# Constant matmuls ahead of the first projection, another order of the first loads, and the norm of x inside a later tile

## The chip, the cores and the metric

The kernel runs on one core of one Trainium2 chip. The metric is the device time of one execution in microseconds (us); several executions are timed, and one more is taken with the hardware profiler. The engines are TensorE (PE, with its weight loads as PEld), VectorE (DVE), ScalarE (ACT), GpSimd (POOL), and SyncE (SP), which issues most transfers.

## The reference, cut to what matters

One encoder block over 512 tokens of 1024 channels. What the change touches is the normalisation of x and the projections that follow it:

```python
def rms_norm(x, g):
    y = xf * lax.rsqrt(jnp.mean(xf * xf, axis=-1, keepdims=True) + EPS)
    return y * g
...
h = rms_norm(x, mix_norm_g[l])
proj = h @ w_in[l]      # mLSTM q, k, v, o, gates | NA q, k, v | memory q | merge gates
...
qk = silu(dwconv3(concat([q_pre, k_pre]), w_conv, b_conv))   # mLSTM branch
```

The rest of the block (mLSTM, neighbourhood attention, attention into 256 memory tokens, gated merge, output projection, a convolutional feed-forward and a last norm) is computed by both kernels alike. All inputs and outputs are float32.

## The kernel before

x is kept transposed: eight k tiles of 128 channels by 512 tokens. Each float32 matmul is made of three in a rounded format (`mm3`, lines 181 to 184): an operand is split into a high part (a rounded copy) and a low part (the difference), and high*high, high*low and low*high are summed in PSUM. `split_act` (186) makes the parts of an activation: the high part on ACT (188), the low part on DVE (189). `emit_split` (153) does so for a block of weights: ACT at 164, DVE at 165. A weight block is up to 1088 columns; `emit_raw` (135) loads it into one of three buffers by SP, and `weights` (170) loads three blocks ahead and splits one ahead. The high and low halves have four buffers each.

The norm is not applied to x before the projection. Only the gain is (`vcol("mix_g", k)`, from the tile `vec`, in which all small vectors stand side by side in 180 columns); the factor per token, 1/rms, is applied to the projection's result. It is formed in two steps. `rstd_cols` (244) reduces the accumulated squares `acc` over partitions by matmuls with a column of ones (249), and takes the power -1/2 on POOL (253); the result is a column `rc`, token by partition. `rstd_row` (256) spreads it over all partitions: eight scalings of the identity on DVE (266), two matmuls (267), and a copy by ACT (269), the tile `rb`.

The start of the program, in source order: SP loads x tile 0, `vec`, block 0 in three pieces (columns 0 to 127, to 511, to 1023; line 142), x tiles 1 to 3, block 1 whole (144); POOL loads `gb`, a small bias; POOL makes constants, and DVE two halved vectors from late columns of `vec` (`mgbh` 239, `ngh` 241). Then comes the loop over the eight k tiles of the first projection, "mlq" (292 to 305): per k tile the twelve matmuls of four feature tiles, each with a PSUM bank of the pool `mm` (`ps_q`). `x_part(k)` (280) splits x tile k, squares it on ACT (283, 286), adds the square to `acc` on POOL (287), and loads x tile k+4. At k = 6 `rstd_cols` is placed ahead of the matmuls, at k = 7 `rstd_row` behind the first feature tile's.

Then four rounds of `conv` (311) and `silu2` (322) treat the four q tiles: DVE multiplies by `rb` (315), ACT and DVE apply the three taps (317 to 319), ACT a tanh (324), DVE 325, and a split. The four feature tiles of k ("mlk") follow, each a `proj` (328) of 24 matmuls into a bank of `mm`, with the same treatment. Next are the token-major blocks ("tm", 369 to 391), whose first and third rounds use the four banks of the second PSUM pool, `at`. The scratch tiles `scr`, seven buffers, hold x tiles, squares and intermediate results.

The source order is not the order on an engine. A scheduler at build time places each instruction on its engine's queue; each queue then runs in order, and each instruction waits for its own inputs.

Of the kernel before, what the change touches and what calls it, by code (L numbers as in the profile page):

```python
# [11 lines left out]
F32 = mybir.dt.float32  # L12
F32R = mybir.dt.float32r
AF = mybir.ActivationFunctionType
# [3 lines left out]
P = 128  # L18
S = 512
D = 1024  # L20
KT = D // P
# [3 lines left out]
FT = DFF // P  # L25
HF = FT // 2
NU = 15
RM, RB = 0.75, 1.4
RATE = (0.85, 1.6, 0)
EPS = 1e-6  # L30
# [65 lines left out]
def hybrid_block(ctx, tc, xT, memT, wflat, vecs, gbias, nabias, outa, outb):  # L96
    nc = tc.nc
    V, A, G, PE, SY = nc.vector, nc.scalar, nc.gpsimd, nc.tensor, nc.sync

    cp = ctx.enter_context(tc.tile_pool(name="cp", bufs=1))  # L100
    wp = ctx.enter_context(tc.tile_pool(name="wp", bufs=3))
    up = ctx.enter_context(tc.tile_pool(name="up", bufs=NU))
    sp = ctx.enter_context(tc.tile_pool(name="sp", bufs=7))
# [7 lines left out]
    def nm(s):  # L111
        uid[0] += 1
        return f"{s}_{uid[0]}"
# [4 lines left out]
    def scr(n=512):  # L118
        return sp.tile([P, 516], F32, tag="scr", name=nm("s"))[:, :n]

    def tiny(n):
        return tp.tile([P, 32], F32, tag="tiny", name=nm("y"), bufs=12)[:, :n]

    def mmps():
        return mmp.tile([P, 512], F32, tag="mm", name=nm("mm"))

    def atps():
        return atp.tile([P, 512], F32, tag="at", name=nm("at"))
# [4 lines left out]
    st = {"raw": 0, "split": 0}  # L133

    def emit_raw(i):
        key, n = BLOCKS[i]
        _, off, _ = BINDEX[key]
        r = wp.tile([P, BW], F32, tag="raw", name=nm("wr"), bufs=3)
        src = wflat[off:off + P * n].rearrange("(p n) -> p n", p=P)
        if i == 0:  # L140
            for a, b in ((0, P), (P, n // 2), (n // 2, n)):
                SY.dma_start(r[:, a:b], src[:, a:b])
        else:
            SY.dma_start(r[:, :n], src)
        raws[i] = r

    def halves(i):
        n, c = BLOCKS[i][1], BCOLS[BLOCKS[i][0][0]](BLOCKS[i][0])
        k = n // c
        k0 = k if n <= HWD else (k + 1) // 2  # L150
        return c, [(0, k0)] + ([(k0, k)] if k0 < k else [])

    def emit_split(i):
        key, n = BLOCKS[i]
        r = raws.pop(i)
        c, hs = halves(i)
        split[i] = []
        for a, b in hs:
            h = wp.tile([P, HWD], F32R, tag="hi", name=nm("wh"), bufs=4)
            l = wp.tile([P, HWD], F32R, tag="lo", name=nm("wl"), bufs=4)  # L160
            m = (b - a) * c
            for u, v in ((0, P), (P, m)) if i == 0 and a == 0 else ((0, m),):
                src = r[:, a * c + u:a * c + v]
                A.activation(h[:, u:v], src, AF.Copy)  # L164
                V.tensor_tensor(l[:, u:v], src, h[:, u:v].bitcast(F32), op=ALU.subtract)  # L165
            for k in range(a, b):
                q = slice((k - a) * c, (k - a + 1) * c)
                split[i].append((h[:, q], l[:, q]))

    def weights(key):  # L170

        i, _, n = BINDEX[key]
        while st["raw"] <= min(i + RAW_AHEAD, len(BLOCKS) - 1):
            emit_raw(st["raw"])
            st["raw"] += 1
        while st["split"] <= min(i + SPLIT_AHEAD, len(BLOCKS) - 1):
            emit_split(st["split"])
            st["split"] += 1
        return split.pop(i)

    def mm3(ps, lh, ll, rh, rl, start, stop):
        PE.matmul(ps, lh, rh, start=start, stop=False)  # L182
        PE.matmul(ps, lh, rl, start=False, stop=False)  # L183
        PE.matmul(ps, ll, rh, start=False, stop=stop)  # L184

    def split_act(h, l, src, scale=1.0):

        A.activation(h, src, AF.Copy, scale=scale)  # L188
        V.scalar_tensor_tensor(l, src, scale, h.bitcast(F32), op0=ALU.mult, op1=ALU.subtract)  # L189


    vec = cp.tile([P, NVEC], F32, name="vec")
    gb = cp.tile([P, 16], F32, name="gb")

    def vcol(name, i):
        o = VEC[name] + i
        return vec[:, o:o + 1]
# [3 lines left out]
    def load_x(k):  # L201
        if k < KT:
            t = scr()
            SY.dma_start(t, xT[:, k, :])
            xk.append(t)

    load_x(0)
    SY.dma_start(vec, vecs)
    emit_raw(0)
    for k in range(1, 4):  # L210
        load_x(k)
    emit_raw(1)
    st["raw"] = 2
    G.dma_start(gb, gbias.partition_broadcast(P))

    ident = cp.tile([P, P], F32, name="ident")
    make_identity(nc, ident)
# [26 lines left out]
    def rstd_cols(acc, ntok, tag, n=D):  # L244

        nt = ntok // P
        ps = atps()
        for t in range(nt):
            PE.matmul(ps[:, t:t + 1], acc[:, t * P:(t + 1) * P], ones[:, 0:1], start=True, stop=True)
        v = tiny(nt)  # L250
        V.tensor_scalar(v, ps[:, :nt], 1.0 / n, EPS, op0=ALU.mult, op1=ALU.add)
        col = cp.tile([P, nt], F32, name=f"rc_{tag}")
        G.tensor_tensor(col, v, nhalf[:, :nt], op=ALU.pow)
        return col

    def rstd_row(col, ntok, tag):

        nt = ntok // P
        ch, cl = tp.tile([P, 32], F32R, tag="tiny", name=nm("y"), bufs=12)[:, :nt], tiny(nt)
        A.activation(ch, col, AF.Copy)  # L260
        V.tensor_tensor(cl, col, ch.bitcast(F32), op=ALU.subtract)
        pb = atps()
        for n, c in enumerate((ch.bitcast(F32), cl)):
            dg = sp.tile([P, 516], F32R, tag="scr", name=nm("s"))[:, :ntok]
            for t in range(nt):
                V.tensor_scalar(dg[:, t * P:(t + 1) * P], ident, c[:, t:t + 1], None, op0=ALU.mult)
            PE.matmul(pb[:, :ntok], onesr, dg, start=n == 0, stop=n == 1)
        rb = cp.tile([P, ntok], F32, name=f"rb_{tag}", tag=f"rb{ntok}", bufs=2 if ntok == S else 1)
        A.activation(rb, pb[:, :ntok], AF.Copy)
        return rb  # L270
# [3 lines left out]
    XH = [hx[k // 4][:, (k % 4) * S:(k % 4 + 1) * S] for k in range(KT)]  # L274
    XL = [hx[2 + k // 4][:, (k % 4) * S:(k % 4 + 1) * S] for k in range(KT)]
    acc = cp.tile([P, S], F32, name="acc_x", tag="acc", bufs=1)
# [2 lines left out]

    def x_part(k):  # L280
        split_act(XH[k], XL[k], xk[k], vcol("mix_g", k))
        if k == 0:
            A.activation(acc, xk[k], AF.Square)
        else:
            sq = scr()
            A.activation(sq, xk[k], AF.Square)
            G.tensor_tensor(acc, acc, sq, op=ALU.add)
        load_x(k + 4)

    x_part(0)  # L290
    done = 1
    for k in range(KT):
        if k % 2 == 0:
            ws = weights(("mlq", k // 2))
        while done < min(KT, k + 1 + (k > 2)):
            x_part(done)
            done += 1
        if k == KT - 2:
            rc = rstd_cols(acc, S, "x")
        wh, wl = ws[k % 2]  # L300
        for f in range(4):
            fs = slice(f * P, (f + 1) * P)
            mm3(ps_q[f], wh[:, fs], wl[:, fs], XH[k], XL[k], k == 0, k == KT - 1)
            if k == KT - 1 and f == 0:
                rb = rstd_row(rc, S, "x")
    rcc = cp.tile([P, NT], F32, name="rcc")
    V.tensor_scalar(rcc, rc, C_ML, None, op0=ALU.mult)

# [16 lines left out]
        V.scalar_tensor_tensor(c, th, 1.0, c, op0=ALU.add, op1=ALU.mult)  # L325
        split_act(dst[0][:, sl], dst[1][:, sl], c)

    def proj(key, XHs, XLs, n=S):
        ws = weights(key)
        ps = mmps()  # L330
        for k in range(KT):
            mm3(ps[:, :n], ws[k][0], ws[k][1], XHs[k], XLs[k], k == 0, k == KT - 1)
        return ps

    qT = [unit(F32R), unit(F32R)]
    kT = [unit(F32R), unit(F32R)]
    for f in range(4):
        silu2(qT, slice(f * S, (f + 1) * S), conv(ps_q[f], rb, "mlw", "mlb", f, 8))
    for f in range(4):
        ps = proj(("mlk", f), XH, XL)  # L340
        silu2(kT, slice(f * S, (f + 1) * S), conv(ps, rb, "mlw", "mlb", 4 + f, 8))

    mh_u, ml_u = unit(F32R), unit(F32R)
# [25 lines left out]
    for c in range(4):  # L369
        if c == 3:  # L370
            mem_part()
        n = 272 if c == 0 else 256
        pss = [(mmps if c % 2 else atps)() for _ in range(NT)]
        for h in range(2):
            ws = weights(("tm", c, h))
            for t in range(NT):
                tsl = slice(t * P, (t + 1) * P)
                for k in range(4):
                    kk = 4 * h + k
                    ps = pss[t][:, :n]  # L380
                    mm3(ps, XH[kk][:, tsl], XL[kk][:, tsl], ws[k][0], ws[k][1], kk == 0, kk == KT - 1)
        for t in range(NT):
            ps = pss[t]
# [418 lines left out]
    for f in range(4):  # L802
        ps = proj(("xaq", f), XH, XL)
# [6 lines left out]
    for f in range(4):  # L810
        ps = proj(("o", f), XH, XL)
# [9 lines left out]
    for f in range(4):  # L821
        ps = proj(("memk", f), MH, ML, M)
# [3 lines left out]
    for i in range(4):  # L826
        ws = weights(("memv", i))
# [10 lines left out]
    for f in range(4):  # L838
        ps = proj(("naq", f), XH, XL)
# [3 lines left out]
    for f in range(4):  # L843
        ps = proj(("nak", f), XH, XL)
# [12 lines left out]
    for br in range(3):  # L857
# [8 lines left out]
        for fp in range(4):  # L866
            tg = []
            for i in range(2):
                f = 2 * fp + i
                ps = proj(("g", br, f), XH, XL)  # L870
# [9 lines left out]
            ws = weights(("br", br, fp))  # L880
            for i in range(2):
                f = 2 * fp + i
                ps = mmps()
# [22 lines left out]
    for f in range(KT):  # L906
        xr = scr()
        SY.dma_start(xr, xT[:, f, :])
        ps = proj(("out", f), GH, GL)
# [73 lines left out]
    for hh in range(2):  # L983
# [3 lines left out]
        for j in range(HF):  # L987
            f = HF * hh + j
            if f == 0:
# [7 lines left out]
                k = KT - 1  # L997
# [19 lines left out]
        for f in range(KT):  # L1017
            ws = weights(("dn", hh, f, 0)) + weights(("dn", hh, f, 1))
            last = hh == 1 and f == KT - 1
            for a, b in ((0, 256), (256, 512)) if last else ((0, 512),):  # L1020
                ps = mmps()[:, :b - a]
# [120 lines left out]
```

## Time and profile before

| | us |
|---|---|
| three timed executions | 917.39, 918.46, 918.47 (median 918.46) |
| the profiled execution | 917.16 |
| its span, first to last instruction | 915.4 |
| DVE, ACT, POOL busy in it | 577.7, 437.7, 135.0 |
| 0 to 10 us: PE busy | 4.55 |
| 10 to 880 us: PE busy | 867.2 |
| 880 to 915.4 us: PE busy | 28.0 |

A timeline row has the start, the duration (of the group, where it says x2 or more, from the first start to the last end), the engine, the line of the kernel, the operation, what it writes and reads with shapes, and, in brackets, how long the engine was idle before it and what ended that. In the rows of groups the busy time and the mean of one instruction stand before the second bar, the idle time of the engine just before them behind it. Matmul durations overlap, so the distance between two starts tells the rate. "fp32r" is the rounded format. `wr` is a raw weight block, `wh` and `wl` its parts, `s` a scratch tile, `u` a large unit tile.

### The profile page before, as it was taken

What the parts mean: (1) busy time and instruction counts of PE and PEld (TensorE: products, weight loads), DVE (VectorE), ACT (ScalarE), POOL (GpSimd) and SP (SyncE); (2) the same over time, 40 slices, a digit from 0 to 9 for tenths busy, and PEclk for the clock granted to TensorE, in tenths of its full rate; (3) what the DMA queues carried; (4) which work ended last, traced back from release to release, by engine and by line L of the source; (5) the groups of instructions that cost most, each with busy time, mean ns of one, the idle gap of its engine ahead of it and who ended that gap; (6) DMA issues with size and microseconds to landing.
All of it is one profiled execution on the core that took longest, in us unless ns stands there. A gap on an engine that the chain in (4) does not pass through costs nothing.

```text
span 915.4 us, 12086 instructions
## 1 busy us (share of the span) xinstructions
PE 899.7 (98%) x4431; PEld 750.8 (82%) x4431; DVE 577.7 (63%) x993; ACT 437.7 (48%) x879; POOL 135.0 (15%) x158
## 2 busy tenths in 40 slices
PE   7999999999999999999999999999999999999996
PEld 5899878888888888788888888888888888888886
DVE  7893665746566668895454548777733477777333
ACT  7464546655545557563334435444422344444442
POOL 6000321102040300111111221111100011111112
PEclk9999999999999999999999999999999999999999
DMA  7223522422231423232223332222222322222322
GB/s 256 96 93 106 189 98 101 155 92 90 81 127 73 134 81 125 83 127 70 93 92 116 137 116 92 92 93 93 85 95 95 115 93 92 93 93 86 95 72 92
DMA packets 32939, 96.39 MB, mean 105 GB/s; under 512 B 4056, under 2 KB 7528, under 8 KB 32880
## 3 DMA queue, kind: packets, MB, share of 16 engines
q1 hardware_dynamic: 31440, 92.45, 29.2%
q0 software_dynamic: 1440, 3.17, 1.2%
q8 instruction: 35, 0.57, 0.3%
q14 instruction: 24, 0.20, 0.1%
HBM read 92.44 MB, written 3.16 MB: 104 GB/s over the span
## 4 chain that ended last, share of the span: by engine, by line
PE 95%; DVE 2%; issue 1%; DMA 0%; ACT 0%; POOL 0%; SPq 0%; POOLq 0%; DVEq 0%; ACTq 0%
PE mm L182 28%; PE mm L183 28%; PE mm L184 28%; PE at L535 2%; PE at L182 2%; PE at L183 2%; PE at L184 2%; PE at L671 1%; PE at L658 1%; DMA wr<-wflat 0%; POOL u L979 0%; PE at L748 0%; PE at L642 0%; PE at L643 0%; DVE s L890 0%
## 5 line engine op out<-in xcount | busy, mean ns | idle before, releaser
L182 PE MATMUL mm<-u,wh 128*128 128x512 f32 (+1 forms) x1115 | 435.8, 391 | 5.4 <-ACT wh L164 5.3
L184 PE MATMUL mm<-u,wl 128*128 128x512 f32 (+1 forms) x1115 | 433.2, 389 | 0.0
L183 PE MATMUL mm<-u,wh 128*128 128x512 f32 (+1 forms) x1115 | 433.0, 388 | 0.0
L164 ACT ACTIVATE wh<-wr 128x512 fp32r<-128x512 f32 (+3 forms) x305 | 189.5, 623 | 298.4 <-PE mm L183 262.6
L165 DVE TENSOR_TENSOR wl<-wr,wh 128x512 fp32r<-128x512 f32 (+3 forms) x305 | 234.4, 770 | 145.2 <-ACT wh L164 141.0
L182 PEld LDWEIGHTS mm<-u,wh 128*128 128x128 f32 x1115 | 209.9, 188 | 50.8 <-ACT wh L164 6.2
L184 PEld LDWEIGHTS mm<-u,wl 128*128 128x128 f32 x1115 | 209.8, 188 | 45.9
L183 PEld LDWEIGHTS mm<-u,wh 128*128 128x128 f32 x1115 | 209.9, 188 | 44.8 <-DVE u L189 0.5
L1012 POOL TENSOR_TENSOR s<-s,rb 128x512 f32<-128x512 f32 x22 | 29.1, 1324 | 266.4 <-DVE s L1011 258.3
L891 POOL TENSOR_TENSOR u<-u,s 128x512 f32<-128x512 f32 x16 | 22.4, 1399 | 166.1 <-DVE s L890 108.9
L188 ACT ACTIVATE u<-s 128x512 fp32r<-128x512 f32 x34 | 21.4, 629 | 52.3 <-DVE s L1015 50.6
L872 DVE TENSOR_TENSOR s<-mm,rb_x 128x512 f32<-128x512 f32 x24 | 16.6, 692 | 28.8 <-PE mm L184 28.8
L189 DVE SCALAR_TENSOR_TENSOR u<-s,u 128x512 fp32r<-128x512 f32 x34 | 23.5, 692 | 14.7 <-ACT u L188 14.4
L523 ACT ACTIVATE E<-R,bi 128x128 f32<-128x128 f32 x80 | 27.8, 394 | 4.7 <-POOL R L504 4.2
L317 ACT ACTIVATE s<-pad,vec 128x512 f32<-128x512 f32 x30 | 24.4, 813 | 8.3 <-DVE pad L315 8.3
L318 DVE SCALAR_TENSOR_TENSOR s<-pad,vec,s 128x512 f32<-128x512 f32 x30 | 22.5, 750 | 6.1 <-ACT s L317 6.1
L182 PE MATMUL mm<-wh,u 128*128 128x256 f32 (+1 forms) x80 | 24.5, 306 | 0.0
L1026 DVE TENSOR_TENSOR u<-mm,u 128x512 f32<-128x512 f32 (+1 forms) x17 | 11.2, 659 | 20.8 <-PE mm L184 20.8
L183 PE MATMUL mm<-wl,u 128*128 128x256 f32 (+1 forms) x80 | 24.3, 304 | 0.0
L184 PE MATMUL mm<-wh,u 128*128 128x256 f32 (+1 forms) x80 | 24.3, 304 | 0.0
L1011 DVE SCALAR_TENSOR_TENSOR s<-s,s 128x512 f32<-128x512 f32 x22 | 15.2, 692 | 13.4 <-ACT s L1010 13.3
L319 DVE SCALAR_TENSOR_TENSOR s<-pad,vec,s 128x512 f32<-128x512 f32 x30 | 22.5, 749 | 0.7
(230 smaller groups left out, 911.1 us busy)
## 6 DMA issues: line engine op xcount, KB each, us to landing
wr<-wflat SPq DMA_DIRECT2D x141, 512.0 KB, 3.2
s<-xT SPq DMA_DIRECT2D x16, 256.0 KB, 4.0
nab<-nabias SPq DMA_DIRECT2D x16, 256.0 KB, 2.7
wr<-wflat SPq DMA_DIRECT2D x17, 192.0 KB, 2.3
R<-rd SPq DMA_DIRECT2D x8, 256.0 KB, 3.5
u<-nav_d POOLq DMA_DIRECT2D x32, 64.0 KB, 3.0
wr<-wflat SPq DMA_DIRECT2D x2, 544.0 KB, 3.2
s<-memT SPq DMA_DIRECT2D x4, 256.0 KB, 3.7
```

The costliest lines, as they stand in the source:

```text
L164: A.activation(h[:, u:v], src, AF.Copy)
L165: V.tensor_tensor(l[:, u:v], src, h[:, u:v].bitcast(F32), op=ALU.subtract)
L182: PE.matmul(ps, lh, rh, start=start, stop=False)
L183: PE.matmul(ps, lh, rl, start=False, stop=False)
L184: PE.matmul(ps, ll, rh, start=False, stop=stop)
L189: V.scalar_tensor_tensor(l, src, scale, h.bitcast(F32), op0=ALU.mult, op1=ALU.subtract)
L317: A.activation(t1, pad[:, 0:512], AF.Identity, scale=vcol(w, i), bias=vcol(b, i))
L318: V.scalar_tensor_tensor(t1, pad[:, 1:513], vcol(w, n + i), t1, op0=ALU.mult, op1=ALU.add)
L319: V.scalar_tensor_tensor(t1, pad[:, 2:514], vcol(w, 2 * n + i), t1, op0=ALU.mult, op1=ALU.add)
L523: A.activation(E[:, i, :], src, AF.Exp, bias=bi[:, d, abs(J - s), s, h:h + 1])
L891: G.tensor_tensor(mgv(f), mgv(f), tg[i], op=ALU.add)
L1012: G.tensor_tensor(c, c, rb2, op=ALU.mult)
```

## The change

Six things are done.

1. A tile `warm` of 128x256 ones is set by DVE, and 13 matmuls of it with itself go into a bank of `at` that nothing reads.
2. The first eight columns of `vec` (the gain of this norm) are loaded by ACT's queue; the other 172 columns by SP behind blocks 0 and 1 and x tiles 0 to 3. `gb` moves from POOL's queue to SP's, behind that.
3. The order on SP is x0, the first two pieces of block 0, x1, the third piece, x2, half of block 1, x3, the other half.
4. The high part of the first 128 weight columns is made by DVE instead of ACT.
5. The square of x tile k is placed behind the split of x tile k+1.
6. `rstd_cols` and `rstd_row` leave the loop over k. They go into the first feature tile of "mlk", behind its k tiles 1 and 7. That tile and the next use banks of `at`, and both stand ahead of the q tiles' convolutions in the source.

```diff
+WARM = 13
...
-        if i == 0:
-            for a, b in ((0, P), (P, n // 2), (n // 2, n)):
-                SY.dma_start(r[:, a:b], src[:, a:b])
-        else:
-            SY.dma_start(r[:, :n], src)
         raws[i] = r
+        if i < 2:
+            cuts = (0, P, n // 2, n) if i == 0 else (0, n // 2, n)
+            return [(r[:, a:b], src[:, a:b]) for a, b in zip(cuts, cuts[1:])]
+        SY.dma_start(r[:, :n], src)
...
-                A.activation(h[:, u:v], src, AF.Copy)
+                if i == 0 and a == u == 0:
+                    V.tensor_copy(h[:, u:v], src)
+                else:
+                    A.activation(h[:, u:v], src, AF.Copy)
...
+    warm = cp.tile([P, 256], F32R, name="warm")
+    V.memset(warm.bitcast(F32), 1.0)
+    pw = atps()
+    for _ in range(WARM):
+        PE.matmul(pw[:, :256], warm[:, :P], warm, start=True, stop=True)
+
+    A.dma_start(vec[:, :8], vecs[:, :8])
+    w0, w1 = emit_raw(0), emit_raw(1)
+    st["raw"] = 2
     load_x(0)
-    SY.dma_start(vec, vecs)
-    emit_raw(0)
-    for k in range(1, 4):
-        load_x(k)
-    emit_raw(1)
-    st["raw"] = 2
-    G.dma_start(gb, gbias.partition_broadcast(P))
+    SY.dma_start(*w0[0])
+    SY.dma_start(*w0[1])
+    load_x(1)
+    SY.dma_start(*w0[2])
+    load_x(2)
+    SY.dma_start(*w1[0])
+    load_x(3)
+    SY.dma_start(*w1[1])
+    SY.dma_start(vec[:, 8:], vecs[:, 8:])
+    SY.dma_start(gb, gbias.partition_broadcast(P))
...
     def x_part(k):
         split_act(XH[k], XL[k], xk[k], vcol("mix_g", k))
+        if k > 0:
+            x_square(k - 1)
+        if k == KT - 1:
+            x_square(k)
+        load_x(k + 4)
+
+    def x_square(k):
         if k == 0:
             A.activation(acc, xk[k], AF.Square)
         else:
             sq = scr()
             A.activation(sq, xk[k], AF.Square)
             G.tensor_tensor(acc, acc, sq, op=ALU.add)
-        load_x(k + 4)
...
+    def proj(key, XHs, XLs, n=S, bank=None, at={}):
+        ws = weights(key)
+        ps = (bank or mmps)()
+        for k in range(KT):
+            mm3(ps[:, :n], ws[k][0], ws[k][1], XHs[k], XLs[k], k == 0, k == KT - 1)
+            if k in at:
+                at[k]()
+        return ps
...
-        if k == KT - 2:
-            rc = rstd_cols(acc, S, "x")
...
-            if k == KT - 1 and f == 0:
-                rb = rstd_row(rc, S, "x")
+
+    ps_k = [proj(("mlk", 0), XH, XL, bank=atps, at={1: lambda: norm.append(rstd_cols(acc, S, "x")),
+                                                    7: lambda: norm.append(rstd_row(norm[0], S, "x"))})]
+    rc, rb = norm
+    ps_k.append(proj(("mlk", 1), XH, XL, bank=atps))
...
-        ps = proj(("mlk", f), XH, XL)
+        ps = ps_k[f] if f < 2 else proj(("mlk", f), XH, XL)
```

More of the change, by code (lines that the diff above doesn't have):

```diff
@@ L287, in x_part @@
             G.tensor_tensor(acc, acc, sq, op=ALU.add)
-        load_x(k + 4)
+    norm = []
+    def proj(key, XHs, XLs, n=S, bank=None, at={}):
[6 more added lines that the diff above has]
+        return ps
     x_part(0)
@@ L326, in silu2 @@
         split_act(dst[0][:, sl], dst[1][:, sl], c)
[L328 to L333, printed above, removed]
     qT = [unit(F32R), unit(F32R)]
```

## The prediction

> **What bounds the kernel now.** I read four views, in this order. First the page: which engine is busy, and whose idle time has a cause.
>
> ```profile
> PE 899.7 (98%) x4431; PEld 750.8 (82%) x4431; DVE 577.7 (63%) x993; ACT 437.7 (48%) x879; POOL 135.0 (15%) x158
> L182 PE MATMUL mm<-u,wh 128*128 128x512 f32 (+1 forms) x1115 | 435.8, 391 | 5.4 <-ACT wh L164 5.3
> ```
>
> TensorE (PE) is busy in 899.7 of 915.4 us, so the change can win only where PE waits or runs slowly; the one long wait is 5.3 us ahead of the first matmul. Then TensorE's timeline at the start:
>
> ```profile
> 5.30 0.80 PE L182 MATMUL mm<-u,wh 128*128 128x512 f32 x1 [5.30 <-ACT wh L164]
> 5.89 0.68 PE L183 MATMUL mm<-u,wh 128*128 128x512 f32 x1
> 6.37 0.63 PE L184 MATMUL mm<-u,wl 128*128 128x512 f32 x1
> 7.14 0.79 PE L182 MATMUL mm<-u,wh 128*128 128x512 f32 x1
> ...
> 9.44 0.58 PE L184 MATMUL mm<-u,wl 128*128 128x512 f32 x1
> 9.86 0.39 PE L182 MATMUL mm<-u,wh 128*128 128x512 f32 x1
> 10.09 0.40 PE L183 MATMUL mm<-u,wh 128*128 128x512 f32 x1
> ```
>
> First column start, second duration. Starts are 0.43 apart until 9.44 and 0.23 from 9.86: TensorE runs at about half rate for its first 4.4 us (the table of windows prints a granted clock of 1.00 there, so only the matmuls' own rows show it). The three matmuls before 7.14 are feature tile 0 of k tile 0; then PE waits for the second piece of the weights. From 7.14 it runs without a wait to 28.79. Third view, the other engines in the same stretch:
>
> ```profile
> 3.70 0.63 ACT L283 ACTIVATE acc_x<-s 128x512 f32<-128x512 f32 x1 [1.69 <-DMA s<-xT]
> 3.92 0.18 DVE L239 TENSOR_SCALAR mgbh<-vec 128x24 f32<-128x24 f32 x1 [3.92 <-DMA vec<-vecs]
> 4.23 0.70 ACT L188 ACTIVATE u<-s,vec 128x512 fp32r<-128x512 f32 x1
> 4.94 0.31 ACT L164 ACTIVATE wh<-wr 128x128 fp32r<-128x128 f32 x1
> 6.57 1.30 ACT L164 ACTIVATE wh<-wr 128x384 fp32r<-128x384 f32 x2 [1.32 <-DMA wr<-wflat]
> ```
>
> The square of x tile 0 stands ahead of its split on ScalarE (ACT); the second weight piece lands at 6.57. Last, the norm's matmuls and VectorE (DVE) under the adds of POOL:
>
> ```profile
> 24.41 0.95 PE L249 MATMUL at<-ones,acc_x 128*128 128x1 f32 x8
> 28.79 0.88 PE L267 MATMUL at<-s,onesr 128*128 128x512 f32 x2
> 13.23 10.12 POOL L287 TENSOR_TENSOR acc_x<-acc_x,s 128x512 f32<-128x512 f32 x6 [1.62 <-ACT s L286]
> 20.42 3.48 DVE L189 SCALAR_TENSOR_TENSOR u<-s,vec,u 128x512 fp32r<-128x512 f32 x2
> ```
>
> **The change, part by part.** *Queue order.* SP issues one load per 0.46 us (three in 1.38). Taking vec out of second place moves the first weight piece from 1.64 to 1.17 and the second from 2.11 to 1.64. With their durations to landing of 3.3 and 4.4 us they land at 4.47 and 6.04 (6.57 before). vec (90 KB) and gb are also out of the way of these bytes; the shortest landing here is 2.7, so the second piece lands between 4.3 and 6.04. I take 6.0, the long end, as all weight rows here took 3.3 or more. It then needs 0.53 on ACT, so feature tile 1 can start at 6.6 instead of 7.14: 0.55 us. Were the landing earlier, tile 0 would bound it: x lands at 3.70, its split is 0.71 on ACT (4.41), the low part 0.75 on DVE (5.2), the copy of 128 columns (now on DVE, 0.28 like the subtraction L165 of that shape) 5.45, the low weights 5.7, and the third matmul ends the group at about 6.1: at most 1.0 us.
>
> The first eight columns of vec go by ACT's queue, 0.42 us for the issue and 4 KB in 32-byte rows, which no row shows; the nearest are 8 KB ones, 1.8 and 3.4 us to landing, so 2.5 to 4.1 against x's 3.70. At worst the split starts 0.4 later, which the wait for the second piece still covers. The ACT table load (1.28 us) moves back by the issue and still ends by 2.5.
>
> Behind these the order is x1, rest of block 0, x2, half of block 1, x3, the other half, vec, gb: x4 is issued at about 5.9 instead of 4.96 and block 2 at 6.4 instead of 5.58. x4 is used at 16.7, block 2 likewise; both land by some 12.5. Two issues more cost 0.9 us of SP, which then waits for the slot of block 0 anyway (8.95). The tight ones are k tile 1 (needed at 8.7): block 0's last piece lands at 7.2 to 7.5, 0.6 on ACT, 0.7 on DVE behind x1's low part gives 8.9 against 9.1; I allow 0.15 us of stall.
>
> *Constant matmuls.* DVE's memset of 128x256 has no row; POOL's 128x400 took 0.43 and DVE's 128x128 ops 0.28, so 0.3 to 0.45; engines are free at 0.74, and PE starts at about 1.3. A 256-column matmul starts every 0.118 at full rate (897.55, 897.66, 897.78), so 0.215 at half: 13 take 1.5 to 2.8 us. At half rate, as every PE start here, they end at about 4.2, ahead of the first real matmul at 4.8 to 5.4. They hide wholly in the 5.3 us wait. If they count towards the 4.4 us of activity that the rate took to rise, it rises at 5.7 to 6.9. The nine matmuls of tiles 1 to 3 took 3.42 us (7.14 to 10.56) and take 9 x 0.232 = 2.09 at full rate: 1.33 us won; at half rate throughout, nothing. I take 1.2, since 0.3 us may still be at half rate.
>
> The Trainium skill's page "TensorE: Matmul & The Clock Gate" (Part 1) says the clock is released only after a free-running window of about 3.4 us that was busy. The row's 4.4 us agrees with that; but by its figure a burst of 2.8 us fills no window, and the 1.2 would be nought: the first rival below.
>
> *The norm.* Eight L249 matmuls (25.22 - 24.41 = 0.81) and two L267 (29.50 - 28.79 = 0.71) are moved, not removed. Of the 0.71, 0.46 is two matmuls' pitch and 0.25 a wait for the diagonal tiles on DVE. The chain between them gets 18 matmuls, 4.14 us, instead of 15, 3.45, so the wait goes: 0.25 us. The squares move one k tile back; acc was complete at 23.35 and is now needed at about 29, so no stall. POOL's adds double DVE's time (0.7 to 1.75 us) and now fall later, when DVE is less urgent: L189 for k tile 6 ended about 22.2, and PE, 2 us earlier, wants it at 22.4. It was the tightest place; I leave 0.1 us.
>
> The reduced row is ready at about 35 instead of 30.3, so the eight convolutions (3.56 us of DVE each, L315 to L189) start 5 us later, and DVE, full from 35 to 58 before (4.98 of 5 us), stays full to about 71. Behind them on DVE are the low weights L165 of the tm blocks. They had 2.1 us in hand (second one done by 63.5, used at 65.7). The two PSUM banks of the k tiles come free at about 48 and 53, wanted at 51.3 and 55.8. So nothing here if the order stays; cover gone, some 0.5 to 1.5 us.
>
> *Sum:* -0.55 - 1.2 - 0.25 + 0.15 + 0.1 = -1.75 us with the 6.04 landing; half the remaining doubt of the landing is up to 0.45 better, so I take **-2.0**. The profiled execution took 917.16 (span 915.4 plus 1.76 around it): 915.2, span 913.4. It is the fastest of four: the others are 917.39, 918.46, 918.47 (median 918.46). The trace does not say what the slower ones lost. A rate that rises 2.6 us later would cost such 1.3 us, and work in the first wait would take that off too. I therefore forecast **915.5**, 0.3 of the 1.3 left in.
>
> **Rivals.** *The clock does not follow.* The constant matmuls end at 4.2, PE idles about a microsecond, and the rate rises only after 4.4 us of real work, at 9.7. For: nothing in the trace shows that a pause is forgiven. Against: PE paused before 7.14 too. From 6.6 to 9.7 there are 7.2 slow matmuls, then 1.8 quick: k tile 1 at 10.1 instead of 10.56. With the norm 0.7 us: 916.5.
>
> *The backlog.* Convolutions 5 us later push L165 behind PE's need between 51 and 75, or the banks late. Against: PE had no wait there. Price 0.5 to 1.5: 916 to 917.
>
> *Other side: DVE held by vec.* L239 and L241 need vec's last columns, now issued tenth (about 4.9) and landing 2.7 to 6.5 later, 7.6 to 11.4. On DVE's queue L239 was first (idle 3.92 us). If it stays ahead of the first L189, the low part of x0 waits: second matmul at about 8.7 to 12.5, k tile 1 at 11.2 to 15 instead of 10.56, so +0.4 to +4.2 with the norm: 917.6 to 921.4. It decides from a landing later than about 7.2. Against: queues are not in source order (the square L283 stands before L188, though written behind it), so L239 is likely set where its data are expected; behind k tile 2's work it costs nothing.
>
> **Chances.** Forecast 0.62; clock 0.15; backlog 0.10; DVE held 0.13. Within 0.2% (1.84 us, what a measurement here can tell from no change) lie 916.6 to 920.3. Faster: forecast 0.62, clock 0.08, backlog 0.05: 0.75. Slower: 0.09 of the held case: 0.09; the rest, 0.16, same. Range 914.0 (earlier landing and no stall) to 917.7, which leaves out most of the held case.
>
> **What would show it.** Right: PE rows of 256 columns from about 1.3; real matmuls 0.23 apart by 7; feature tile 1 before 6.7; L267 followed by a full-pitch start; L239 on DVE after some L189 and without a long idle. Wrong: starts 0.43 apart past 8; idle DVE on vec; new PE waits between 50 and 75; a span above 915.

## The result, and the profile after

| | before | changed |
|---|---|---|
| median of 22 executions, us | 917.98 (916.61 to 918.48) | 916.69 (915.06 to 917.75) |
| profiled execution, us | 917.16 | 916.63 |
| its span, us | 915.4 | 914.8 |
| first real matmul, us | 5.30 | 5.73 |
| matmuls 0.23 apart from, us | 9.86 | 9.67 |
| k tile 1 begins, us | 10.56 | 10.37 |

The changed kernel takes 0.9985 of the time of the kernel before (95% interval 0.9979 to 0.9991): 1.3 us less, inside the 0.2% that the prediction called no change. The forecast was 915.5 for the time, and 2.0 us less (915.2) for an execution like the profiled one; the two profiled executions differ by 0.53 us.

The page of the changed kernel, TensorE's load and its group of matmuls:

```profile
PE 902.2 (99%) x4444; PEld 753.9 (82%) x4444; DVE 578.1 (63%) x995; ACT 437.0 (48%) x878; POOL 135.4 (15%) x157
L185 PE MATMUL mm<-u,wh 128*128 128x512 f32 (+1 forms) x1099 | 428.8, 391 | 1.4 <-ACT u L191 1.4
```

The 13 constant matmuls are in the count. The long wait of 5.3 us is a wait of 1.4 us now, but a wait for something else: not the weights' split but x's split on ACT. The timeline of TensorE at the start:

```profile
1.18 3.14 PE L215 MATMUL at<-warm 128*128 128x256 f32 x13 [1.18 <-DVE warm L212]
5.73 1.65 PE L185 MATMUL mm<-u,wh 128*128 128x512 f32 x3 [1.40 <-ACT u L191]
7.17 0.63 PE L186 MATMUL mm<-u,wh 128*128 128x512 f32 x1
...
8.88 0.63 PE L186 MATMUL mm<-u,wh 128*128 128x512 f32 x1
9.30 0.53 PE L187 MATMUL mm<-u,wl 128*128 128x512 f32 x1
9.67 0.40 PE L185 MATMUL mm<-u,wh 128*128 128x512 f32 x1
9.91 0.39 PE L186 MATMUL mm<-u,wh 128*128 128x512 f32 x1
```

Two things are to be seen. The first real matmul comes 0.43 us later than before, not earlier. And the real matmuls are at half rate until 9.67, as if nothing had run ahead of them. The timeline of ACT says where the first comes from:

```profile
0.73 0.40 ACTq L217 DMA_DIRECT2D vec<-vecs  x1
3.66 1.28 ACT L191 ACT_TABLE_LOAD   x1 [3.66 <-DMA s<-xT]
4.95 0.72 ACT L191 ACTIVATE u<-s,vec 128x512 fp32r<-128x512 f32 x1
5.58 0.51 ACT L167 ACTIVATE wh<-wr 128x384 fp32r<-128x384 f32 x1
```

The table load, which ran at 0.73 in the kernel before, stands behind the landing of x tile 0. In the compiled order of ACT, the first activation is now the split, which has two inputs from transfers (x and the eight columns of vec); the table load ahead of it carries the wait for x. Before, the first activation was the square, which needs x alone, and its table load had no wait. That the second input is the reason is a reading that fits every trace here; no run tests it by itself. So 1.28 us are on the path from x to the first matmul.

It is not the later place of the squares in the source (part 5) that put the split first. e4 below has parts 5 and 6 without the new start, and its square still came first, with the table load at 0.73; e10 has the squares in their old place, and its table load came late:

```profile
0.73 1.28 ACT L290 ACT_TABLE_LOAD   x1 [0.73 <-PEq L1144]
3.95 1.28 ACT L191 ACT_TABLE_LOAD   x1 [3.95 <-DMA s<-xT]
```

The first row is e4's, the second e10's. What e10 shares with the changed kernel is the start, in which the gain has a transfer of its own.

The norm's two groups on TensorE, where the second took 0.88 us before:

```profile
31.14 0.95 PE L265 MATMUL at<-ones,acc_x 128*128 128x1 f32 x8
36.19 0.63 PE L283 MATMUL at<-s,onesr 128*128 128x512 f32 x2
```

The next matmul starts at 36.66, 0.47 us after the start of the second group, against 0.71 before: the wait of 0.24 us is gone.

### The profile page after: what moved, and what is told of

It is laid out like the page before. It is cut to its first block, busy times and chain, and to the rows that moved or that the text cites. A ratio compares the mean times of both kernels' runs of the same rounds, so it can differ in the third digit from the quotient of the medians.

```text
span 914.8 us, 12115 instructions
## 1 busy us (share of the span) xinstructions
PE 902.2 (99%) x4444; PEld 753.9 (82%) x4444; DVE 578.1 (63%) x995; ACT 437.0 (48%) x878; POOL 135.4 (15%) x157
## 4 chain that ended last, share of the span: by engine, by line
PE 95%; DVE 2%; issue 1%; ACT 1%; POOL 0%; DMA 0%; POOLq 0%; DVEq 0%; ACTq 0%
PE mm L185 28%; PE mm L186 28%; PE mm L187 28%; PE at L185 2%; PE at L186 2%; PE at L187 2%; PE at L562 2%; PE at L698 1%; PE at L685 1%; POOL u L1006 0%; PE at L775 0%; PE at L669 0%; DMA s<-xT 0%; PE at L670 0%; DVE s L917 0%
## 5 line engine op out<-in xcount | busy, mean ns | idle before, releaser
L185 PE MATMUL mm<-u,wh 128*128 128x512 f32 (+1 forms) x1099 | 428.8, 391 | 1.4 <-ACT u L191 1.4
L187 PE MATMUL mm<-u,wl 128*128 128x512 f32 (+1 forms) x1099 | 427.0, 389 | 0.0
L186 PE MATMUL mm<-u,wh 128*128 128x512 f32 (+1 forms) x1099 | 426.6, 388 | 0.0
L167 ACT ACTIVATE wh<-wr 128x512 fp32r<-128x512 f32 (+1 forms) x304 | 189.1, 623 | 296.9 <-PE mm L186 264.1
L185 PEld LDWEIGHTS mm<-u,wh 128*128 128x128 f32 x1099 | 206.9, 188 | 45.6 <-ACT u L191 1.7
L187 PEld LDWEIGHTS mm<-u,wl 128*128 128x128 f32 x1099 | 206.8, 188 | 45.3
L186 PEld LDWEIGHTS mm<-u,wh 128*128 128x128 f32 x1099 | 207.0, 188 | 44.2 <-DVE u L192 0.3
L1053 DVE TENSOR_TENSOR u<-mm,u 128x512 f32<-128x512 f32 (+1 forms) x17 | 11.2, 660 | 20.8 <-PE mm L187 20.8
```

## The experiments

Each was timed against the kernel before on the same chip (its median was 917.76 to 917.81 there, and 917.98 beside the changed kernel). "Under 916" counts executions below 916.0 us; the last three columns are from the profiled execution, in us, the last but one being where starts get 0.23 apart.

| kernel | median | ratio (95%) | under 916 | first real matmul | full rate from | k tile 1 |
|---|---|---|---|---|---|---|
| changed | 916.69 | 0.9985 (0.9979 to 0.9991) | 6 of 22 | 5.73 | 9.67 | 10.37 |
| e1_table | 915.92 | 0.9981 (0.9972 to 0.9989) | 6 of 11 | 4.67 | 9.72 | 9.96 |
| e2_nowarm | 917.47 | 1.0000 (0.9991 to 1.0009) | 0 of 11 | 5.86 | 9.24 | 10.41 |
| e3_warm20 | 915.48 | 0.9975 (0.9965 to 0.9985) | 8 of 8 | 5.76 | 6.75 | 8.83 |
| e4_norm_only | 917.53 | 0.9997 (0.9988 to 1.0006) | 0 of 11 | 5.86 | 11.44 | 11.15 |
| e5_table_warm18 | 915.26 | 0.9972 (0.9962 to 0.9983) | 8 of 8 | 5.08 | 5.72 | 8.61 |
| e6_table_nowarm | 916.69 | 0.9988 (0.9980 to 0.9997) | 2 of 11 | 4.57 | 10.18 | 10.18 |
| e7_warm16 | 915.23 | 0.9976 (0.9967 to 0.9985) | 8 of 10 | 5.75 | 6.76 | 8.86 |
| e8_start_only | 919.48 | 1.0018 (1.0009 to 1.0027) | 0 of 11 | 5.81 | (see below) | 10.49 |
| e9_start_warm16 | 918.28 | 1.0010 (1.0002 to 1.0019) | 0 of 11 | 4.76 | 7.55 | 8.96 |
| e10_squares_own | 917.14 | 0.9992 (0.9983 to 1.0001) | 2 of 11 | 6.02 | 10.29 | 10.98 |

### The table load taken off the path

```diff
     A.dma_start(vec[:, :8], vecs[:, :8])
+    tl = cp.tile([P, 1], F32, name="tl")
+    G.memset(tl, 1.0)
+    A.activation(tl, tl, AF.Square)
```

> One square of a 128x1 constant tile is put on ACT right behind its DMA issue, so that ACT's table load (1.28 us) no longer stands behind the landing of x tile 0. Theory A (the table load on the path, and the 1.4 us pause of PE behind the constant matmuls, ate the gain): the first split starts at about 3.7 instead of 4.95, the first real matmul at 4.4 to 4.5 instead of 5.73, the pause is under 0.4 us, real matmuls start 0.23 apart by 7, k tile 1 begins at 8.4 to 8.8 instead of 10.37: 1.5 to 2 us less than the changed kernel, about 915.0. Rival B (the constant matmuls don't count, the rate rises at about 9.6 whatever stands before): starts 0.43 apart until 9 or later, k tile 1 at about 9.6: 0.5 to 0.8 us less, about 916.0.

ACT's timeline in this kernel:

```profile
1.17 1.28 ACT L220 ACT_TABLE_LOAD   x1 [1.17 <-PEq L1163]
2.46 0.20 ACT L220 ACTIVATE tl<-tl 128x1 f32<-128x1 f32 x1
3.90 0.72 ACT L191 ACTIVATE u<-s,vec 128x512 fp32r<-128x512 f32 x1 [1.24 <-DMA vec<-vecs]
```

The split starts 1.05 us earlier, the first real matmul 1.06 us (4.67): this half of theory A holds. The other half doesn't hold as expected: the time is B's. In the profiled execution there is a pause of 0.35 us ahead of the first real matmul and 0.36 us more between 5.10 and 5.46, in which PE waits for x's low part, and the starts stay 0.43 apart until 9.47. B's reason, a fixed moment near 9.6, falls with the table above: full rate came at 5.72 to 11.44.

### Without the constant matmuls

```diff
-    warm = cp.tile([P, 256], F32R, name="warm")
-    V.memset(warm.bitcast(F32), 1.0)
-    pw = atps()
-    for _ in range(WARM):
-        PE.matmul(pw[:, :256], warm[:, :P], warm, start=True, stop=True)
```

> The changed kernel without the constant matmuls and their memset. Theory A (they count, but only in those executions in which the pause is forgiven): the median rises by 0.5 to 1 us to about 917.4, and no execution is near 915.2. Rival B (they don't count): the same 916.7 with the same spread of 915.1 to 917.7.

The median rises by 0.78 us, and no execution is near 915.2: theory A. The changed kernel's executions fall into two groups: six of 22 lie around 915.2, some 2.2 us under the median without the 13 matmuls, the others around 916.9, some 0.6 under it. The profiled execution is one of the others, so no trace shows one of the six.

### More of them

```diff
-WARM = 13
+WARM = 20
```

> 20 constant matmuls instead of 13, so that they end at about 5.7 (7 more at 0.22) where the first real matmul starts. Theory A: no pause, the rate has risen by 7 at the latest, k tile 1 at 9.0 to 9.3 instead of 10.37, about 915.5 in every execution. Rival B: the rate rises at about 9.6 all the same, 916.7.

```diff
-WARM = 13
+WARM = 16
```

> 16 constant matmuls, table load left late: they end at about 5.0, with a pause of 0.7 us. Theory C (a stretch of about 3.4 us without a pause, whose place in the program differs from execution to execution): 3.8 us of work instead of 3.1, so about half of the executions near 915.3 and the others near 916.7 (with 13 it was 6 of 22 near 915.3); spread over 1.3 us. Rival E (only an end at the first real matmul counts): as with 13, a quarter near 915.3, median 916.7.

TensorE's timeline with 16:

```profile
1.18 3.45 PE L215 MATMUL at<-warm 128*128 128x256 f32 x16 [1.18 <-DVE warm L212]
5.75 1.17 PE L185 MATMUL mm<-u,wh 128*128 128x512 f32 x3 [1.12 <-ACT u L191]
6.76 0.40 PE L186 MATMUL mm<-u,wh 128*128 128x512 f32 x1
7.00 0.39 PE L187 MATMUL mm<-u,wl 128*128 128x512 f32 x1
```

With 20 all executions lie within 0.82 us, at 915.13 to 915.95. With 16 eight of ten do as well, more than the half expected, and rival E falls: here the constant matmuls end 1.12 us ahead of the first real one, and the rate stays up across that pause. 16 took 3.45 us here and 3.78 in e9 below, where 13 took 3.14: in e7 the rate rose inside the burst. What goes with an early rise in these runs is the length of the burst: 3.1 us is enough in a quarter of the executions, some 3.5 to 3.8 in most, 4.63 (20 matmuls) in all, and so is the 4.05 of 18 in e5 below. With 18 and 20 the burst also lasts until the real matmuls begin, so for those two the length and the missing pause are not told apart.

### Both at once, and the table load alone

The edits are those of e1 with WARM = 18, and of e1 with that of e2.

> The early table load and 18 constant matmuls, which end at about 5.3 (13 ended at 4.32; 5 more at 0.22). Theory C (the rate rises only after a stretch of PE work without a pause, so that even the 0.35 us pause and the wait for x's low part, 0.4, spoiled it in part of the executions with 13): no pause, starts 0.23 apart by 7, k tile 1 at 8.2 to 8.6, all executions within 0.9 us of each other, median 914.8 to 915.2, some 0.5 below the 915.48 with 20 and the late table load. Rival: the table load no longer matters once PE is covered by constant matmuls (x tile 1, landed at 7.1, is then the bound): 915.4 to 915.6.

> The early table load without constant matmuls. Theory A for the table load by itself: the first real matmul at 4.6 instead of 5.86, but at half rate up to about 8 to 11, so of the 1.2 us about half is left: median 916.7 to 917.0 against 917.47 without either. Rival (the half rate takes all of it): 917.4.

With the constant matmuls long enough, the early table load adds nothing to the median that can be told apart (915.26 against 915.23 and 915.48). That is what the rival said, but 915.26 lies between its range and theory C's, and k tile 1 (8.61) and the spread of 0.43 us are as C had them: undecided between the two. TensorE's and ACT's timelines of e5 show the next bound:

```profile
8.61 0.50 PE L185 MATMUL mm<-u,wh 128*128 128x512 f32 x1 [0.40 <-ACT wh L167]
```

```profile
7.92 0.63 ACT L167 ACTIVATE wh<-wr 128x512 fp32r<-128x512 f32 x1 [0.62 <-DMA wr<-wflat]
```

The rival named x tile 1; it is the third piece of block 0, which lands at 7.9. Without constant matmuls the early load is worth 0.78 us (916.69 against 917.47), as expected.

### The norm alone, and the start alone

e4 is the kernel before with parts 5 and 6 of the change. e8 is the changed kernel with `x_part`, the loop of the first projection and `proj` of the kernel before; e9 is e8 with e1's edit and WARM = 16.

```diff
     def x_part(k):
         split_act(XH[k], XL[k], xk[k], vcol("mix_g", k))
-        load_x(k + 4)
+        if k > 0:
+            x_square(k - 1)
+        if k == KT - 1:
+            x_square(k)
+        load_x(k + 4)
...
-        if k == KT - 2:
-            rc = rstd_cols(acc, S, "x")
...
-            if k == KT - 1 and f == 0:
-                rb = rstd_row(rc, S, "x")
...
+    ps_k = [proj(("mlk", 0), XH, XL, bank=atps, at={1: lambda: norm.append(rstd_cols(acc, S, "x")),
+                                                    7: lambda: norm.append(rstd_row(norm[0], S, "x"))})]
```

> The kernel before with only the norm's part of the change: squares one k tile later, the norm inside the first k feature tile, that tile and the next in the other PSUM pool. By the prediction's step: 0.25 us less than before, 917.7, with the wait ahead of the second spreading matmul gone and no new wait of PE up to 120 us. Rival C (the convolutions' backlog costs as much): 918.0 or more, with a PE wait between 50 and 75 us.

> The changed kernel with the norm as before (squares with their own k tile, the two norm steps inside the loop of the first projection). If the norm's part is worth 0.25 us in this company too: median 916.9 to 917.0, with a wait of 0.25 us ahead of the second spreading matmul. Rival (the later adds of POOL matter in the faster start): more than 917.3, with a wait of PE for a low part on DVE at k tile 5 or 6.

> The norm as before, with the early table load and 16 constant matmuls: the faster start without the norm's move. Theory F (the loss of the start alone, 919.48, is PE waiting for the accumulated squares, whose adds on POOL are not earlier than in the kernel before): PE gains some 1.5 us at the start and loses it again ahead of the norm's first matmuls, a wait of 1.5 to 2.5 us there; 917.5 to 919. Rival G (the loss is the clock's fall behind the pause of 1.5 us): no fall with 16, the wait stays under 1 us, 916.0 to 916.5.

e4 came out 0.28 us under the kernel before, with no new wait of PE; the interval holds no change, and the trace has the 0.24 us. Its first real matmul is late (5.86) because the first weight piece, loaded in the order of before, landed at 5.50 in the profiled execution. e8 was a surprise: the start by itself is slower than the kernel before. Its waits of TensorE have a new one, and its windows show something else, in the last column but two, the granted clock:

```profile
PE at L265 <- POOL acc_x L303: 1.0, 1, 1.0
```

```profile
7.00:8.00 1.00, 1.00 (x6) 0.76 (x5) 0.29 (x1) 0.33 (x1) 0.00 (x0) 0.89 0.98 315
8.00:9.00 1.00, 1.00 (x4) 0.81 (x3) 0.66 (x2) 0.92 (x3) 0.00 (x0) 0.50 1.03 387
9.00:10.00 1.00, 1.00 (x3) 0.78 (x3) 0.95 (x3) 1.00 (x2) 0.00 (x0) 0.50 1.12 323
10.00:11.00 1.00, 1.00 (x4) 0.74 (x3) 1.00 (x2) 1.00 (x3) 0.07 (x1) 0.50 0.98 354
11.00:12.00 1.00, 1.00 (x6) 0.84 (x5) 0.82 (x2) 0.98 (x2) 1.00 (x1) 0.90 0.97 365
```

The rate had risen in this execution (starts 0.23 apart from 6.94 to 7.64) and fell again to one half for 3.4 us. The 0.89 and 0.90 at its ends put it from 7.78 to 11.2. PE had idled 1.49 us behind the constant matmuls and 0.29 us before 6.60. In e7, 1.12 us of idling did not bring it down.

The new wait is on the accumulated squares. ACT's timeline in e8 says why they are late:

```profile
13.80 1.15 ACT L167 ACTIVATE wh<-wr 128x512 fp32r<-128x512 f32 x2
16.34 0.63 ACT L167 ACTIVATE wh<-wr 128x512 fp32r<-128x512 f32 x1 [1.39 <-PE mm L186]
16.87 0.62 ACT L302 ACTIVATE s<-s 128x512 f32<-128x512 f32 x1
```

The square of k tile 3 stands behind a weight split that waits for PE to free its buffer. In the kernel before, the same square, the third of the seven that are added on POOL, ran ahead of any such split:

```profile
14.03 0.62 ACT L286 ACTIVATE s<-s 128x512 f32<-128x512 f32 x1
```

Five adds follow on POOL at 1.6 us each in e8, and the sum is complete at 25.7 instead of 23.35; PE wants it at 24.8. e9 tells the two causes apart, as its timeline of TensorE shows:

```profile
25.03 1.05 PE L268 MATMUL at<-ones,acc_x 128*128 128x1 f32 x8 [1.47 <-POOL acc_x L306]
```

The clock does not fall at the start of that execution, k tile 1 begins 1.53 us earlier than in e8, and the wait has grown to 1.47 us; the median is 918.28, in theory F's range and far from G's. An earlier start only brings PE sooner to a sum that POOL finishes no earlier than 25.

The clock is not out of it, though. The mean granted clock of each execution beside the experiments is on record: in the kernel before none was under 0.996, in e8 three of 11 were (0.993 to 0.995) and in e9 three (0.995). In e9 the five executions at 0.998, like the profiled one, took 917.49 to 918.02 us, the other six 918.28 to 919.58. So a fall of the clock seems to add about a microsecond in some executions, but no trace of e9 shows it or its place. The wait alone is enough against G: even the five are over 917.4.

### The squares put back

```diff
     def x_part(k):
         split_act(XH[k], XL[k], xk[k], vcol("mix_g", k))
-        if k > 0:
-            x_square(k - 1)
-        if k == KT - 1:
-            x_square(k)
+        x_square(k)
         load_x(k + 4)
```

> The changed kernel with each square put back to its own k tile; the two norm steps stay in the first k feature tile. Theory F: the squares' place is worth little, since the sum is now wanted 5 us later: 916.5 to 917.0, no PE wait ahead of the norm's first matmuls. Rival H (the delay of the squares itself frees ACT and DVE at the start): above 917.3, k tile 1 or later waiting on ACT or DVE.

Inconclusive: 917.14 is between the two expectations, the interval overlaps that of the changed kernel, and in the profiled execution x tile 0 landed 0.29 us later (3.95), which moves everything behind it. PE has no wait ahead of the norm's first matmuls, as F said.

## Why the prediction came out as it did

**The sign and the range held; the size was about half.** The forecast 915.5 is 2.5 us under the median of before (917.98), and 2.0 us was its sum for one execution; 1.3 us came. By the prediction's own classes that is "same", to which it gave 0.16, and not "faster" (0.75). That the time lies inside the range is partly luck: the main term did not come about in most executions, and the range was wide enough for that. Its sign of being wrong, starts 0.43 apart past 8, showed. The terms, from medians:

| term of the sum | predicted | measured |
|---|---|---|
| queue order | -0.55 | -0.06 (e2 against e4) |
| constant matmuls, the clock | -1.2 | -0.78 (changed against e2) |
| norm, alone | -0.25 | -0.28 (e4), 0.24 in the trace |
| stalls at k tiles 1 and 6 | +0.25 | no such wait in the trace; 0.40 at k tile 1 in e5, where the start is faster |

The measured terms are differences of medians, partly from different sessions, and the interval of each ratio is about 0.8 us to either side. So -0.06 and -0.28 cannot be told from nothing, and the size of -0.78 is loose: by the ratios (0.9985 against 1.0000) it would be -1.4. What the traces show of each term is the firmer part.

**The step that failed** is in the part on the queue order: the table load "moves back by the issue and still ends by 2.5". It ended at 4.94. The pieces did land earlier: the second weight piece was split at 5.58 instead of 6.57. But x's split started at 4.95, and e1 and e6 show that the table load alone makes that 1.05 us. In e6, where it runs early, the medians give the order 0.84 us (916.69 against e4's 917.53), inside the predicted 0.55 to 1.0.

**The clock's term failed in most executions: the rival that was given 0.15 is what they do.** The prediction let 13 matmuls, ended at 4.2, count across a pause of a microsecond towards a rise at 5.7 to 6.9. In the profiled execution the rate rose at 9.67, as "the clock does not follow" had it (9.7), and its 916.5 is near the median. In six of 22 the forecast's case came true, judged by their times near 915.2. The page "TensorE: Matmul & The Clock Gate" of the Trainium skill (Part 1) lets the clock rise only after a free-running window of 3.4 us that was busy. The runs bear it out: a burst of 3.1 us rarely suffices and a longer one does, and the half rate of e8 lasted 3.4 us. The page's other rule there, that the clock falls after an idle window, does not cover e8: its clock fell when PE had idled about 1.7 us of the 3.4 us ahead of it.

**The pause was lengthened by the table load.** The prediction put the first real matmul at 4.8 to 5.4; it came at 5.73, and the pause was 1.4 us instead of 0.6 to 1.2. The burst's own length seems to matter more than the pause: e7 (a longer burst, a pause of 1.12) is under 916 in eight of ten, e1 (13 matmuls, a pause of 0.35) in six of eleven, and of these six some owe it to the early table load, since e6 has two of eleven without any constant matmuls.

**The norm was right for the wrong company.** The prediction priced its move at the wait that the kernel before shows. Beside the faster start it is worth more: without it (e8) the median is 2.8 us above the changed kernel's. The prediction said that the sum, complete at 23.35, would be wanted at 29; it did not ask what happens if it is wanted at 24.8. From the trace, 0.95 us of this are the wait for the sum, 0.24 the other wait, and some 0.4 the fall of the clock; the token-major stage begins 1.84 us later (55.09 against 53.25). The remaining 1 us between medians is open: that profiled execution was one of the quicker ones (918.64), and three of the others had a lower mean clock (0.993 to 0.995 against its 0.996), which no trace explains.

**The other rivals fell.** DVE was not held: `mgbh` was queued behind four low parts of x and ran at 11.12 without a wait. The backlog came without a price, as the table of windows of the changed kernel shows:

```profile
50.00:60.00 10.00, 10.00 (x69) 9.38 (x68) 9.85 (x16) 6.57 (x12) 0.00 (x0) 1.00 0.32 107
60.00:70.00 10.00, 10.00 (x84) 10.00 (x83) 10.00 (x21) 7.55 (x14) 1.87 (x2) 1.00 0.16 54
70.00:75.00 5.00, 5.00 (x44) 5.00 (x44) 4.13 (x16) 2.74 (x6) 0.00 (x0) 1.00 0.53 164
```

The columns after the stretch and its length are busy time (and count) of PE, PEld, DVE, ACT and POOL. DVE is full to 70, as predicted (71), and PE has no wait.

**The spread.** The kernel before varies by 1.9 us, the changed one by 2.7, e3 by 0.8 and e5 by 0.4, the last two over eight executions each. With the long burst most of the spread is gone, which suggests that it was the moment at which the rate rises; the prediction had only guessed that, and no trace of a slow and a quick execution of one kernel shows it.

The quickest versions are e5, e3 and e7 (0.9972, 0.9975 and 0.9976 of the time before), which cannot be told apart; e5 is the steadiest.

## What to carry to other kernels

Look at what becomes the first instruction of an engine when loads are reordered: with the square first, the table load ran ahead of all data; once the split came first, the table load stood behind x. Matmuls that are to raise the clock should be a burst of the length that the runs ask for (4.05 us and more here, in all of 16 executions), not as many as fit before the data land; a burst that is a little too short wins only now and then, and one that holds up the first real work a little (0.4 us in e5 against e1) can cost less than it saves. A faster start paid here only once the next thing that TensorE waits for was moved out of its way in the same step.

## What the runs showed of the hardware that was not expected

- A table load on ACT can carry a wait of the activation behind it: 1.28 us came behind the landing of x (3.66 to 4.94), though the same load ran at 1.17 in e1, before x was there.
- TensorE's rate fell back to one half for 3.4 us (e8, 7.78 to 11.2) after pauses of 1.49 and 0.29 us; after one of 1.12 us (e7) it stayed up.
- The half rate at the very start is not in the granted clock, which reads 1.00 there; only the later fall is (0.50). At the start the distance between matmuls has to be read.
